# A hybrid attention and state-space layer: normalising the inputs before the conditioning is known, and a written order for the first two query units

## The chip, the core and the metric

One core of a Trainium2 chip runs the whole kernel. The metric is the device time of one launch in microseconds, the median of several runs.

## The reference, cut to what matters

The kernel computes one layer of a diffusion backbone over 1024 latent tokens of width 1024 and 256 context tokens. The part that the change touches is the start: the conditioning vector gives a shift and a scale per channel, the inputs are RMS-normalised and modulated, and the result is projected to queries, keys and values.

```
mod = (silu(c) @ ada_w + ada_b)
sh1, sc1, g1, sh2, sc2, g2 = split(mod, 6)
y = x * rsqrt(mean(x * x) + EPS)
h = (y * norm1_w) * (1.0 + sc1) + sh1
p = h @ w_in            # queries, keys, values, gates, state-space inputs
```

Everything behind it (rotary embedding, neighbourhood attention, a state-space scan in both directions, output projection, gated MLP with a depthwise convolution, final norm) is the same in both kernels.

## The kernel before, in words

All tensors are kept with the channels on the partitions: the input x is 8 channel tiles of 128 by 1024 tokens (`xt`), loaded in two halves of 512 tokens. Matrices are float32. For the large products each operand is split into a high part (`hh`, `wh`, in the fp32r format) and a low part (`hl`, `wl`: the rest), and three products (high by high, high by low, low by high) are added in PSUM.

The start has five kinds of work.

- **Norm.** ScalarE squares the 8 tiles of a half (L150, tiles `sq_x`), VectorE adds them up (L152, `sqa_x`), TensorE sums over the partitions (L154, `stat_x`). `rstd_rows` (L93) takes the root and the reciprocal, and a product with a matrix of ones (L105) spreads the inverse norm over the partitions in PSUM (`rbt`, one bank for each half).
- **Conditioning.** The product of the two conditioning vectors (latent and context) with `ada_w` is made in eight blocks of 256 columns. A block (`ada`, L157) loads 1 MB of weights (L159, `adaw`), makes eight products (L163, `adap`), copies the result to SBUF on ScalarE (L166, `adas`), and brings it onto the partitions with two small products (L169, `mp`). VectorE adds the bias (L172, `mod`, `modc`). Blocks 4 to 7 are scales, 0 to 3 shifts. A scale and a shift block together give the constants of a **pair** of channel tiles (L192, `scl`).
- **Modulation.** For each pair and half, `norm` (L174) makes `ny` = x times scale times inverse norm on VectorE (L176), `hh` = `ny` plus shift on ScalarE (L177) and `hl` = `ny` plus shift minus `hh` on VectorE (L178).
- **Weights.** `load_w` (L75) loads 512 KB for a unit of 128 output columns (`ws`), rounds it to `wh` on ScalarE (L79) and takes the rest `wl` on VectorE (L80).
- **Units.** `fm_unit` (L237) makes one unit: 8 channel tiles, three products each, two halves of 512 tokens, so 48 products (L90, `fu_qk`). There are eight query and key units. The products of `early` units run tile by tile as `hh` and `hl` become ready.

Nothing in the code fixes the order between these kinds: a scheduler places each engine's instructions when the program is built, and each engine then takes its own in that order. The weight loads of the conditioning have 4 buffers (`adap`), so that the loads of the last blocks wait for products of the first. All loads of the start are issued from one queue, SyncE's.

```
        for i in range(4):
            ada(4 + i)
            if i == 0:
                load_x(1)
            ada(i)
            if i < 3:
                pre[i] = load_w(A["wf"][8 + i], KT, P, f"qk0{i}")
```

## Time and profile before

| | |
|---|---|
| median of 3 runs | 1399.26 us (1398.8 to 1403.24) |
| the profiled execution | 1398.01 us |
| its span on the core | 1396.3 us |
| TensorE busy (matmuls) | 1330.7 us, 95% |
| VectorE, ScalarE, GpSimd busy | 854.9, 627.9, 307.9 us |
| share of the chain that ended last | TensorE 78%, DMA 8%, VectorE 5%, ScalarE 4% |

The chain that ended last is followed back from the last instruction, at each step to what released it. The first 60 us hold the work that the change touches. A line "x4" stands for four instructions that follow each other; the bracket at its end is the time for which the engine stood idle before it, and what ended that.

### The profile page before, as it was taken

The page shows a single profiled execution, that of the slowest core. Times are in us where ns is not written, and L with a number is a line of the kernel's source. Part 1 is how long each engine was busy: PE and PEld are TensorE (multiplying, and loading weights), DVE is VectorE, ACT ScalarE, POOL GpSimd, SP SyncE. Part 2 cuts the span into 40 slices and gives each one's busy share as a digit, 9 for nine tenths or more (in the row PEclk, how much of TensorE's full clock was granted, in tenths as well). Part 3 has the DMA queues.
Part 4 walks back from the last instruction along what each step waited for, and adds up shares of the span by engine and source line. Part 5 has one row for each costly group of instructions (what it writes and reads, how often), then busy time and mean ns, then how long its engine had stood idle before and what let it go on. Part 6 is the DMA issues. An engine that isn't in the chain of part 4 may idle for free.

```text
span 1396.3 us, 20022 instructions
## 1 busy us (share of the span) xinstructions
PE 1330.7 (95%) x7539; PEld 1118.8 (80%) x7539; DVE 854.9 (61%) x1343; ACT 627.9 (45%) x1052; POOL 307.9 (22%) x297
## 2 busy tenths in 40 slices
PE   5999999999989999999989999999999998999996
PEld 3788998889878787777887888888888877878885
DVE  5684246742377766548877655565656685585663
ACT  5441224332155558536646443454444554364441
POOL 0010000023657852000222222222222111201210
PEclk9999999999999999999999999999999999999998
DMA  9564675521697687343858676766667777677772
GB/s 370 217 166 123 162 238 196 192 91 49 190 256 207 206 228 255 107 138 119 201 119 198 160 187 153 176 159 150 162 156 174 235 245 187 160 219 206 186 179 74
DMA packets 118160, 251.02 MB, mean 180 GB/s; under 512 B 11944, under 2 KB 37288, under 8 KB 116784
## 3 DMA queue, kind: packets, MB, share of 16 engines
q1 hardware_dynamic: 92576, 197.58, 44.4%
q0 software_dynamic: 25488, 52.18, 20.1%
q8 instruction: 59, 0.97, 0.3%
q14 instruction: 37, 0.30, 0.1%
HBM read 212.16 MB, written 37.55 MB: 179 GB/s over the span
## 4 chain that ended last, share of the span: by engine, by line
PE 78%; DMA 8%; DVE 5%; ACT 4%; issue 2%; POOL 2%; SPq 0%; DVEq 0%; POOLq 0%; ACTq 0%
PE u L871 28%; PE pd L90 8%; PE fu_qk L90 6%; PE fu_x L90 6%; PE tu_v L90 4%; PE tu_z L90 3%; PE oc L90 3%; PE av L666 2%; PE os L90 2%; PE pm L1040 2%; PE pt L648 2%; PE oa L90 1%; DMA seg<-cum_d 1%; PE s L627 1%; PE fu_c L90 1%
## 5 line engine op out<-in xcount | busy, mean ns | idle before, releaser
L871 PE MATMUL u<-op,whu 128*128 128x512 f32 (+1 forms) x760 | 227.2, 382 | 1.7 <-DVE op L827 0.9
L871 PEld LDWEIGHTS u<-op,whu 128*128 128x128 f32 x760 | 140.1, 190 | 32.6 <-DVE op L827 1.1
L863 ACT ACTIVATE whu<-as 128x512 fp32r<-128x512 f32 x115 | 67.7, 625 | 173.9 <-PE u L871 166.0
L844 POOL DMA_DIRECT2D as<-in_w_up x69 | 66.3, 988 | 357.5 <-DMA as<-in_w_up 153.7
L871 PE MATMUL u<-op,wlu 128*128 128x512 f32 (+1 forms) x380 | 144.0, 380 | 0.0
L871 PE MATMUL u<-opx,whu 128*128 128x512 f32 (+1 forms) x384 | 110.2, 378 | 1.7 <-ACT whu L863 1.1
L864 DVE TENSOR_TENSOR wlu<-as,whu 128x512 fp32r<-128x512 f32 x115 | 76.0, 686 | 25.9 <-ACT whu L863 25.7
L871 PEld LDWEIGHTS u<-op,wlu 128*128 128x128 f32 x380 | 72.1, 190 | 14.9
L871 PEld LDWEIGHTS u<-opx,whu 128*128 128x128 f32 x384 | 69.6, 188 | 17.7 <-ACT whu L863 2.9
L90 PE MATMUL pd<-opx,wh_dn 128*128 128x512 f32 x256 | 81.3, 399 | 0.7 <-ACT wh_dn L79 0.6
L894 DVE TENSOR_TENSOR xa<-u,yz 128x512 f32<-128x512 f32 (+1 forms) x24 | 15.5, 646 | 98.2 <-PE u L871 98.2
L871 PE MATMUL u<-opx,wlu 128*128 128x512 f32 (+1 forms) x192 | 71.7, 376 | 0.0
L639 ACT ACTIVATE pr<-pr,mx 128x640 f32<-128x640 f32 x64 | 52.8, 825 | 39.3 <-DVE mx L638 39.2
L638 DVE CUSTOM_DVE_ANT_0 pr<-s,tabt 128x640 f32<-128x640 f32 x64 | 52.0, 818 | 20.2 <-PE s L628 16.1
L666 PE MATMUL av<-pts,vp 128*64 128x128 f32 x640 | 55.3, 285 | 5.8 <-ACT pts L650 5.3
L851 POOL DMA_DIRECT2D yz<-in_w_up x46 | 53.8, 1202 | 31.1 <-ACT yz L850 29.5
L90 PEld LDWEIGHTS pd<-opx,wh_dn 128*128 128x128 f32 x256 | 47.8, 189 | 12.6 <-ACT wh_dn L79 1.4
L871 PE MATMUL u<-opz,whu 128*128 128x512 f32 (+1 forms) x192 | 56.3, 376 | 1.2 <-ACT yz L886 1.2
L650 ACT ACTIVATE pts<-pt 128x640 f32<-128x640 f32 x64 | 43.8, 695 | 29.9 <-PE pt L648 19.7
L666 PEld LDWEIGHTS av<-pts,vp 128*64 128x64 f32 x640 | 40.5, 139 | 18.4 <-ACT pts L650 8.6
L648 PE MATMUL pt<-cst,pr 128*128 128x128 f32 x320 | 48.6, 283 | 5.5 <-ACT pr L639 2.6
L90 PE MATMUL pd<-opx,wl_dn 128*128 128x512 f32 x128 | 50.8, 398 | 1.9 <-DVE wl_dn L80 1.8
(644 smaller groups left out, 3574.8 us busy)
## 6 DMA issues: line engine op xcount, KB each, us to landing
as<-in_w_up SPq DMA_DIRECT2D x69, 256.0 KB, 4.0
as<-in_w_up POOLq DMA_DIRECT2D x69, 256.0 KB, 3.9
yz<-in_ada_wt SPq DMA_DIRECT2D x32, 512.0 KB, 4.5
ws_dn<-in_w_down SPq DMA_DIRECT2D x32, 448.0 KB, 4.0
as<-in_w_up SPq DMA_DIRECT2D x23, 512.0 KB, 5.8
yz<-in_w_up POOLq DMA_DIRECT2D x46, 256.0 KB, 5.8
g_d<-xa POOLq DMA_DIRECT2D x22, 512.0 KB, 4.6
tabt<-in_tab SPq DMA_DIRECT2D x48, 192.0 KB, 5.2
```

Source lines behind the costliest of these rows:

```text
L90: pe.matmul(out[:, t0:t1], st(a, k), mv(b, k, t0, t1), start=k == 0 and p == 0, stop=k == kend - 1 and p == 2, **kw)
L638: dve.tensor_tensor_reduce(pr, ps[:, lo:lo + 640], tabt[m % 2][:, 384 * j:384 * j + 640], -1.0, BIG, OP.add, OP.min, mx)
L639: act.activation(pr, pr, AF.Exp, bias=mx, scale=-1.0, accum_out=sm[:, n % 8:n % 8 + 1])
L648: pe.transpose(pt[:, i * P:(i + 1) * P], pr[:, i * P:(i + 1) * P], ident)
L650: act.activation(pts, pt[:, 0:640], AF.Copy)
L666: pe.matmul(av[64 * j:64 * j + 64, cb], vt, pp[j][:, i * P:(i + 1) * P], start=i == 0, stop=i == 4, skip_group_check=True)
L844: pool.dma_start(t, d, accum_op=OP.add)
L851: pool.dma_start(t, d, accum_op=OP.add)
L863: act.activation(h, src, AF.Copy)
L864: dve.tensor_tensor(l, src, f32(h), OP.subtract)
L871: mm = pe.matmul(ps[:, t0:t1], aops[n, o][a][:, k], bops[o][b][:, k, t0:t1], start=first and o < 5 and (t0 == 0 or n == 2), stop=end, skip ...
L1040: pe.matmul(dst[o], aops[n, o][a][:, k], sops[o][b][:, k], start=k == i == 0 and (o in (0, 2, 4) or o > 4 and first), stop=k == 3 and i == ...
```

## The change

1. `unit` multiplies the tiles of a half by the inverse norm in place, all eight at once and before the conditioning is needed (L214 of the changed kernel). The modulation is then `hh` = scale times y plus shift in one ScalarE instruction (L221); a second ScalarE instruction takes the shift off again (`nt`, L222), and VectorE makes `hl` = y times scale minus `nt` (L223). A negated shift (`neg`, L198) is added for it.
2. The first two query units are taken out of the loop. Their products are issued in pieces of one pair and one half (`query`, six products), and `in_turn` makes every TensorE instruction of the start follow the one written before it: the order on TensorE is the order of the text.
3. The conditioning loads are issued by `ada_load` in a written order, in six buffers. The tiles `ch` and `cl` of the context are allocated later.
4. The third unit's weights, and later ones, are loaded and split after the last conditioning load and the last `hh` and `hl`.

```diff
--- before.py
+++ after.py
@@ -108,19 +108,15 @@
...
-    ch = hxc.tile([P, KT, TC], FR, name="ch")
-    cl = hxc.tile([P, KT, TC], FR, name="cl")
...
-        adap = p0.enter_context(tc.tile_pool(name="adap", reuse_waits="tile", bufs=4))
+        adap = p0.enter_context(tc.tile_pool(name="adap", reuse_waits="tile", bufs=6))
...
+        def ada_load(i):
+            for b in (4 + i, i):
+                adaw[b] = adap.tile([P, KT, 256], FP, tag="ada", name=f"adaw{b}")
+                held["load"] = sp.dma_start(adaw[b], A["ada_w"][b]).ins
...
+        ada_load(0)
...
+        def mm(*a, **kw):
+            last[0] = pe.matmul(*a, **kw).ins
+
+        def in_turn(fn, *a):
+            if last[0] is None:
+                return fn(*a)
+            with tc.issue_after(last[0]):
+                return fn(*a)
...
-        def norm(src, rb, a, b, oh, ol, kt, n, key):
-            y = wk0.tile([P, n], FP, tag=f"ny{n // P}", name=f"ny_{key}{kt}", bufs=n // P)
-            dve.scalar_tensor_tensor(y, src[:, kt], a, rb, OP.mult, OP.mult)
-            act.activation(oh[:, kt], y, AF.Identity, bias=b)
-            dve.scalar_tensor_tensor(ol[:, kt], y, b, f32(oh[:, kt]), OP.add, OP.subtract)
...
+        def shift_scale(i):
+            for b in (4 + i, i):
+                in_turn(ada, b)
+            dve.tensor_scalar(neg[:, 2 * i:2 * i + 2], mod[:, 2 * i:2 * i + 2], -1.0, None, OP.mult)
...
+        def unit(h):
+            c = halves[h]
+            for kt in range(KT):
+                dve.tensor_tensor(xh[h][:, kt], xh[h][:, kt], rbt[:, c], OP.mult)
+
+        def norm(i, h):
+            c = halves[h]
+            for kt in (2 * i, 2 * i + 1):
+                y, a, b = xh[h][:, kt], scl[:, 0, kt:kt + 1], mod[:, kt:kt + 1]
+                t = wk0.tile([P, 512], FP, tag="nt", name=f"nt_x{h}{kt}", bufs=4)
+                held["high"] = act.activation(hh[:, kt, c], y, AF.Identity, scale=a, bias=b).ins
+                act.activation(t, f32(hh[:, kt, c]), AF.Identity, bias=neg[:, kt:kt + 1])
+                held["low"] = dve.scalar_tensor_tensor(hl[:, kt, c], y, a, t, OP.mult, OP.subtract).ins
+
+        early = [mmp.tile([P, T], FP, tag="mm", name=f"fu_qk0{u}") for u in range(2)]
+
+        def query(u, i, h):
+            wt, c = pre[u], halves[h]
+            for k in (2 * i, 2 * i + 1):
+                for p, (a, b) in enumerate(((0, 0), (0, 1), (1, 0))):
+                    mm(early[u][:, c], wt[a][:, k], (hh, hl)[b][:, k, c], start=k == 0 and p == 0,
+                       stop=k == KT - 1 and p == 2)
...
+        rows(0)
+        shift_scale(0)
+        pre[0] = load_w(A["wf"][8], KT, P, "qk00")
+        load_x(1)
+        ada_load(1)
+        unit(0)
+        norm(0, 0)
+        queries((0,), 0, (0,))
+        shift_scale(1)
+        pre[1] = load_w(A["wf"][9], KT, P, "qk01")
+        ada_load(2)
+        rows(1)
+        norm(1, 0)
+        queries((0,), 1, (0,))
+        queries((1,), 0, (0,))
+        unit(1)
+        norm(0, 1)
+        queries((1,), 1, (0,))
+        ada_load(3)
+        shift_scale(2)
+        norm(1, 1)
+        queries((0, 1), 0, (1,))
+        norm(2, 0)
+        queries((0, 1), 1, (1,))
+        norm(2, 1)
+        shift_scale(3)
+        queries((0, 1), 2, (0, 1))
+        for h in range(2):
+            norm(3, h)
+        queries((0, 1), 3, (0, 1))
+        with after("load", "high", "low"):
+            pre[2] = load_w(A["wf"][10], KT, P, "qk02")
...
-                pq.append(fm_unit(wt, hs, T, mmp, "mm", f"qk{blk}{f2}"))
+                pq.append(early[f2] if blk == 0 else fm_unit(wt, hs, T, mmp, "mm", f"qk{blk}{f2}"))
```

The order that the scheduler then gives each engine is shown at three places. **VectorE**, from the end of the first half's norm (`dg`) on. Before:

```order
L101 TENSOR_TENSOR dg_x_152<-cst,rst_x_149 128x512
L172 TENSOR_TENSOR mod<-mp_168,vec 128x2
L172 TENSOR_TENSOR modc<-mp_168,vec 128x2
L192 SCALAR_TENSOR_TENSOR scl<-mod,vec 128x2
L192 SCALAR_TENSOR_TENSOR scl<-modc,vec 128x2
L176 SCALAR_TENSOR_TENSOR ny_x_203<-xt,scl,rbt 128x512
L176 SCALAR_TENSOR_TENSOR ny_x_207<-xt,scl,rbt 128x512
```

In the changed kernel (the rows of the second half's sums, `sqa_x_274`, that stand between are part of it):

```order
L101 TENSOR_TENSOR dg_x_154<-cst,rst_x_151 128x512
L214 TENSOR_TENSOR xt<-xt,rbt 128x512 x8
L191 TENSOR_TENSOR mod<-mp_168,vec 128x2
L191 TENSOR_TENSOR modc<-mp_168,vec 128x2
L80 TENSOR_TENSOR wl_qk_194<-ws_qk_192,wh_qk_193 128x1024
L173 TENSOR_TENSOR sqa_x_274<-sqa_x_274,sq_x_276 128x512
L191 TENSOR_TENSOR mod<-mp_184,vec 128x2
L191 TENSOR_TENSOR modc<-mp_184,vec 128x2
L201 SCALAR_TENSOR_TENSOR scl<-mod,vec 128x2
L201 SCALAR_TENSOR_TENSOR scl<-modc,vec 128x2
L173 TENSOR_TENSOR sqa_x_274<-sqa_x_274,sq_x_279 128x512
L198 TENSOR_SCALAR neg<-mod 128x2
```

Behind these stand four more sums and then the first `hl`. Eight multiplications and one weight split moved ahead of the first scale. **TensorE**, from the second conditioning block's sums on; before (`fu_qk_448` and `fu_qk_497` are the first two units):

```order
L169 MATMUL mp_266<-sel,adas_264 128x2 x2
L163 MATMUL adap_273<-adaw_271,sc 32x256 x8
L90 MATMUL fu_qk_497<-hh,wh_qk_290 128x512
L90 MATMUL fu_qk_448<-hh,wh_qk_196 128x512
L90 MATMUL fu_qk_448<-hl,wh_qk_196 128x512
L90 MATMUL fu_qk_497<-hh,wh_qk_290 128x512
L90 MATMUL fu_qk_497<-hl,wh_qk_290 128x512
L169 MATMUL mp_284<-sel,adas_282 128x2 x2
L163 MATMUL adap_315<-adaw_313,sc 32x256 x8
```

In the changed kernel (`fu_qk_121` is the first unit):

```order
L158 MATMUL fu_qk_121<-hh,wl_qk_194 128x512
L158 MATMUL adap_228<-adaw_202,sc 32x256 x8
L158 MATMUL mp_239<-sel,adas_237 128x2 x2
L158 MATMUL adap_244<-adaw_204,sc 32x256 x8
L158 MATMUL mp_255<-sel,adas_253 128x2 x2
L158 MATMUL stat_x_273<-ones_63,sqa_x_274 128x1 x4
L158 MATMUL fu_qk_121<-hh,wh_qk_193 128x512
L105 MATMUL rbt<-dg_x_304,cst 128x512
L158 MATMUL fu_qk_121<-hl,wh_qk_193 128x512
```

Where unit products stood between a block's eight products and the two small ones that need its copy, the two now follow each other. **ScalarE**, around the copies of the third pair's blocks in the changed kernel:

```order
L221 ACTIVATE hh<-xt,mod,scl 128x512 x2
L222 ACTIVATE nt_x_335<-hh,neg 128x512
L221 ACTIVATE hh<-xt,mod,scl 128x512
L222 ACTIVATE nt_x_339<-hh,neg 128x512
L221 ACTIVATE hh<-xt,mod,scl 128x512
L222 ACTIVATE nt_x_388<-hh,neg 128x512
L222 ACTIVATE nt_x_392<-hh,neg 128x512
L185 ACTIVATE adas_362<-adap_353 128x256
```

Eight passes over the second half's first two pairs now stand ahead of the copy `adas_362`. Behind the query and key units the engines' order is the same in both kernels but for a stretch of the MLP's up-projection, where groups of 512 and 256 columns (line 871, `u`) change places.

## Rows read from the trace of the kernel before

**Rows 1.** The page, part 1: busy time of each engine.

```profile
PE 1330.7 (95%) x7539; PEld 1118.8 (80%) x7539; DVE 854.9 (61%) x1343; ACT 627.9 (45%) x1052; POOL 307.9 (22%) x297
```

**Rows 2.** Busy time by stretch: stretch, length, each engine, granted clock, DMA share, GB/s.

```profile
0.00:11.70 11.70, 0.00 (x0) 0.00 (x0) 5.21 (x10) 7.38 (x11) 0.20 (x4) 1.00 0.83 301
11.70:34.30 22.60, 17.11 (x98) 10.15 (x98) 13.63 (x28) 11.17 (x20) 0.00 (x0) 1.00 1.01 404
34.30:57.50 23.20, 23.16 (x156) 17.39 (x156) 17.15 (x38) 7.42 (x14) 0.00 (x0) 1.00 0.63 248
57.50:140.00 82.50, 82.50 (x396) 68.58 (x396) 50.31 (x64) 28.47 (x51) 5.72 (x8) 1.00 0.56 148
```

**Rows 3.** The same view, first 57.5 us, the units' products (fu_qk) alone.

```profile
0.00:57.50 57.50, 19.17 (x73) 13.30 (x74) 0.00 (x0) 1.00 0.82 320
```

**Rows 4.** The chain that ended last, from 55 us: start, length, what.

```profile
57.52 17.79 PE fu_qk L90 x76
```

**Rows 5.** Timeline of TensorE: start, length, line, operation, count, idle before.

```profile
11.70 1.86 PE L154 MATMUL stat_x<-ones,sqa_x 128*128 128x1 f32 x8 [11.70 <-DVE sqa_x L152]
13.50 1.93 PE L163 MATMUL adap<-adaw,sc 128*32 128x256 f32 x16
15.36 2.08 PE L105 MATMUL rbt<-dg_x,cst 128*128 128x512 f32 x2
...
20.86 1.93 PE L163 MATMUL adap<-adaw,sc 128*32 128x256 f32 x16 [2.78 <-DMA adaw<-in_ada_w]
25.36 1.02 PE L169 MATMUL mp<-sel,adas 128*128 128x2 f32 x4 [2.56 <-ACT adas L166]
26.52 1.84 PE L154 MATMUL stat_x<-ones,sqa_x 128*128 128x1 f32 x8
...
30.75 1.78 PE L105 MATMUL rbt<-dg_x,cst 128*128 128x512 f32 x2
...
32.80 1.07 PE L163 MATMUL adap<-adaw,sc 128*32 128x256 f32 x16
...
41.52 1.07 PE L163 MATMUL adap<-adaw,sc 128*32 128x256 f32 x16
...
47.51 0.50 PE L169 MATMUL mp<-sel,adas 128*128 128x2 f32 x4
```

**Rows 6.** Timeline of VectorE, the same columns.

```profile
6.14 5.51 DVE L152 TENSOR_TENSOR sqa_x<-sqa_x,sq_x 128x512 f32<-128x512 f32 x7 [4.93 <-ACT sq_x L150]
...
18.12 0.16 DVE L172 TENSOR_TENSOR mod<-mp,vec 128x2 f32<-128x2 f32 x1 [3.26 <-PE mp L169]
...
24.55 1.22 DVE L80 TENSOR_TENSOR wl_qk<-ws_qk,wh_qk 128x1024 fp32r<-128x1024 f32 x1
...
28.98 0.69 DVE L101 TENSOR_TENSOR dg_x<-cst,rst_x 128x512 f32<-128x512 f32 x1
...
39.61 2.74 DVE L178 SCALAR_TENSOR_TENSOR hl<-ny_x,mod,hh 128x512 fp32r<-128x512 f32 x4
...
42.65 2.72 DVE L176 SCALAR_TENSOR_TENSOR ny_x<-xt,scl,rbt 128x512 f32<-128x512 f32 x4
```

**Rows 7.** Timeline of ScalarE, the same columns.

```profile
38.35 2.57 ACT L177 ACTIVATE hh<-ny_x,mod 128x512 fp32r<-128x512 f32 x4 [0.95 <-DVE mod L172]
42.72 0.38 ACT L166 ACTIVATE adas<-adap 128x256 f32<-128x256 f32 x1 [1.80 <-PE adap L163]
```

**Rows 8.** Transfers issued from 33 to 34.3 us: count, size, us to landing.

```profile
adaw<-in_ada_w SPq DMA_DIRECT2D x1, 1024.0 KB, 10.3
```

**Rows 9.** Busy time by stretch (columns of rows 2) at the MLP's start.

```profile
702.00:704.00 2.00, 2.00 (x12) 2.00 (x11) 2.00 (x5) 0.18 (x1) 0.86 (x1) 0.50 1.00 208
```

**Rows 10.** Timeline of TensorE in the up-projection.

```profile
710.92 0.38 PE L871 MATMUL u<-op,whu 128*128 128x256 f32 x1 [0.40 <-ACT op L826]
...
712.18 0.39 PE L871 MATMUL u<-op,whu 128*128 128x256 f32 x1 [0.88 <-DVE op L827]
...
714.35 1.03 PE L871 MATMUL u<-opx,whu 128*128 128x256 f32 x4 [0.60 <-ACT whu L863]
```

More of the change, by code (lines that the diff above doesn't have):

```diff
@@ L168, in ada @@
             for f in range(2):
[L169 removed]
+                mm(mp[:, f], sb[:, f * P:(f + 1) * P], sel, start=True, stop=True)
             c0 = 2 * b
@@ L193, in hymba @@
                                          vec[:, V_N1 + 2 * i:V_N1 + 2 * i + 2], OP.add, OP.mult)
-            for h in range(2):
-                if i == 0 and h:
-                    rstd_rows(mmp, wk0, stats(wk0, xh[1], 4, "x1"), 4, "mm", "x1", "sqa4", rb=rbx[1])
-                for kt in (2 * i, 2 * i + 1):
-                    c = slice(512 * h, 512 * h + 512)
-                    norm(xh[h], rbx[h], scl[:, 0, kt:kt + 1], mod[:, kt:kt + 1], hh[:, :, c], hl[:, :, c], kt, 512, f"x{h}")
+        rbt = mmp.tile([P, T], FP, tag="mm", name="rbt")
@@ new lines, in hymba, with rows @@
+        halves = [slice(512 * h, 512 * h + 512) for h in range(2)]
+        def rows(h):
+            sums = in_turn(stats, wk0, xh[h], 4, f"x{h}")
+            rstd_rows(mmp, wk0, sums, 4, "mm", f"x{h}", "sqa4", rb=rbt[:, halves[h]])
+        def unit(h):
[10 more added lines that the diff above has]
+                held["low"] = dve.scalar_tensor_tensor(hl[:, kt, c], y, a, t, OP.mult, OP.subtract).ins
@@ L201, in hymba @@
+    cl = hxc.tile([P, KT, TC], FR, name="cl")
     hs = (hh, hl)
@@ L286, in hymba @@
             for f2 in range(2):
-                wt = pre[2 * blk + f2] if 2 * blk + f2 in pre else load_w(A["wf"][8 + 2 * blk + f2], KT, P, f"qk{blk}{f2}")
+                wt = pre.get(2 * blk + f2)
+                if not wt:
+                    with after("load", "high", "low"):
+                        wt = load_w(A["wf"][8 + 2 * blk + f2], KT, P, f"qk{blk}{f2}")
                 wts.append(wt)
-                pq.append(fm_unit(wt, hs, T, mmp, "mm", f"qk{blk}{f2}"))
+                pq.append(early[f2] if blk == 0 else fm_unit(wt, hs, T, mmp, "mm", f"qk{blk}{f2}"))
             pA, pB = pq
```

39 lines of the change are left out of this document (20 added, 19 removed).

## The prediction, made blind

> **What bounds the kernel now.** I read the views from the whole to the part. The page says that TensorE works for 95% of the span [rows 1], so the first question is where it does not. The busy time by stretch answers for the start [rows 2]: nothing until 11.70 us, 17.11 of 22.60 us until 34.3, then 23.16 of 23.20 and 82.50 of 82.50. From 34.3 us to 140 us TensorE has no gap worth naming, and from 57.5 us on it does nothing but units and what belongs to them. So the change can win only what TensorE idles before 34.3 us: the first 11.70 us wait for the first half's sums, which the change leaves alone, and 22.60 - 17.11 = 5.5 us lie behind them. Anything that opens a gap behind 34.3 us is lost in full, because the chain that ended last runs through these very products [rows 4].
>
> By 57.5 us 73 of the units' products are done [rows 3], beside all eight conditioning blocks. The scheduler gets there by putting products of the first two units between a block's eight products and the two small ones that need its copy: the block at 41.52 us has its `mp` only at 47.51 us, and TensorE works in between [rows 5].
>
> **What is removed.** The loads of the last conditioning block are issued near 34 us and land 10.3 us later [rows 8], near 44 us. In the new order all eight stand ahead of the third unit's weights. The queue moves 404 GB/s in 11.70 to 34.3 us [rows 2], so a block of 1.05 MB takes 2.6 us; x, eight blocks and two weights are about 13.6 MB, which ends near 38 us (an estimate from that rate). The first pair's second block can start behind the first block's `mp` instead of at 20.86 us after a wait of 2.78 us for its load [rows 5]. That wait and the 2.56 us for its copy go; they are most of the 5.5 us.
>
> **What is added, step by step.** I walk TensorE in its new order, with row durations. Until 17.4 us (the end of `rbt`, 15.36 + 2.08 [rows 5]) nothing changes.
> - *First product.* Block 4's `mp`, block 0, its copy and `mp` are done by about 21.2 us, with 0.5 us of waiting for the copy. But the first `hh` needs `scl`, and on VectorE eight multiplications by the norm stand ahead of it. The nearest rows are the `ny` passes, which also read PSUM: four in 2.72 us, 0.66 us each [rows 6]. So 8 x 0.66 = 5.3 us, then `wl` 1.22, one sum 0.7 and five tiny operations 0.5: 17.4 + 7.7 = 25.1 us. `hh` takes 0.7 [rows 7]. The first product starts at 25.8 us: **4.6 us of waiting**.
> - *Second product.* It needs `hl`, and in the written order nothing may pass it. Ahead of `hl` VectorE has five sums, each bound to the one before (seven took 5.51 us, 0.79 each [rows 6]), then `hl` itself, 0.7: 25.2 + 4.7 = 29.9 us at the most, 29.1 if the sums go at their bare 0.7. TensorE is free at 26.3: **3.0 us**.
> - *Blocks 5 and 1.* Block, copy, `mp`, block, copy, `mp` now follow each other. A copy is 0.38 us and starts 0.13 us behind its block (42.72 against 41.52 + 1.07) [rows 5, 7], and the product behind it follows at 0.1: 0.6 us, twice: **1.2 us**. The same for blocks 7 and 3: **1.2 us**, and for block 2: **0.5 us**.
> - *Second half's norm.* From the end of `stat_x` at 28.36 us to the end of `dg` at 29.67 us it took 1.3 us [rows 5, 6], beneath a conditioning block. Now one unit product (with 0.3 us of its own wait) stands there, and the root stands behind two `hh` on ScalarE: **1.9 us**.
> - *Block 6.* Its copy stands behind eight ScalarE passes, `hh` and `nt`. Four `hh` take 2.57 us [rows 7], so eight end 4.9 us behind the first multiplied tile of the second half, near 48 us, where TensorE has done its 17 products (17.79 us for 76, 0.234 each [rows 4]) and the block by about 46.4: **1.8 us**.
>
> The sum is 0.5 + 4.6 + 3.0 + 1.2 + 1.2 + 0.5 + 1.9 + 1.8 = 14.7 us of waiting, against 5.5: **9.2 us more**. A second working gives nearly the same: conditioning ends near 60.3 us instead of 57.5, with 48 products done (6, 18 and 24 by the written order) instead of 73: 2.8 + 25 x 0.234 = 8.7 us.
>
> **What comes for nothing.** The sixteen `nt` passes are 16 x 0.62 = 9.9 us of ScalarE, which works for 18.6 of the 45.8 us between 11.7 and 57.5 us [rows 2]; the part on the path is the 1.8 us above. The later loading of the third unit's weights stays beneath the products of pair 3; without that cover it would cost the split, 1 + 1.2 us. Rope and context work are placed alike. `hh` now has a scale in memory beside its bias, which no row shows; I take the row of `hh` with a bias alone, with nothing and twice its 0.7 us as ends.
> The Trainium skill, ScalarE: Activation LUTs, What ACT_TABLE_LOAD costs, puts about 93 ns on each per-partition operand; by that the eight passes ahead of block 6's copy, four of them `hh`, and the first `hh` would add some 0.5 us, and the sum would be 9.7 us. No row of this trace shows it.
>
> **The clock.** The granted clock reads 1.00 in these stretches [rows 2], but the same block takes 1.93 us at 13.50 and 20.86 and 1.07 us at 32.80 [rows 5]. I read the early rows as the lower of the two levels, 1.2 GHz, and those from 32.8 us on as 2.4 GHz; ahead of the rise TensorE worked without a gap from 26.5 us. In the new order its longest unbroken work before 40 us is about 4 us (29.1 to 33.3). Either that is enough: then the second half's `stat_x` and `rbt` come at the high level, each some 0.9 us less, and five more unit products at the low one, 0.2 us each: -0.8, in all +8.4. Or the rise waits for the dense products behind 42 us: block 1 costs 0.9 more and twelve products 0.2 each, while block 6's wait shrinks by 1.8 because TensorE comes later itself: +1.5, in all +10.7. I take +9.5 between the two, as the rows don't tell them apart.
>
> **The up-projection.** Groups of `u` change places there. The waits near by are 0.40, 0.88 and 0.60 us [rows 10]: 1.9 us either way, taken as nothing.
>
> **The sum.** The profiled execution took 1398.01 us, of which 1396.3 are the span. 1398.0 + 9.5 = 1407.5. The median of the three runs lies 1.25 us above that execution, so I forecast 1408.8 us.
>
> **The rivals.**
> *The waits close up (faster).* Nothing but TensorE's own work need limit it once the loads are there. If `hl` came with `hh` and each copy hid beneath something, the start would lose only its first 11.70 us, and the gain is the old 5.5 us: 1393.8 us. For it speak the earlier loads. Against it stands the order itself: eight multiplications ahead of the first scale, five sums ahead of the first `hl`. It decides at the first `hl`: faster needs the new waits to stay under 1.3 us in all (5.5 less 4.2), and the first product alone has 4.6. I give it 6%.
> *Half of it (no change).* If VectorE takes its multiplications faster than the `ny` rows and TensorE is at the high level from the start, the first two waits shrink to half (3.8 less), the low level's cost goes (some 4 us, as three blocks, two sums and a spread each give back 0.9), and 1 to 3 us are left: about 1401. 15%.
> *The clock falls back (slower still).* At the MLP's start a stretch of 2 us shows the granted clock at 0.50 with TensorE busy throughout [rows 9], behind gaps of the kind that the new order puts around blocks 6, 2, 7 and 3. Each such time would cost half its length, 1 to 2 us here, two of them up to 4: 1412 us. 17%.
> The Trainium skill, TensorE: Matmul & The Clock Gate, Why this matters for your kernels, warns of just this: gaps between bursts of matmuls send the engine back to its lower level.
> *The change does not do what it says.* The order on TensorE is written and shows in the built program, so this has no chance of its own.
>
> **How the numbers follow.** 0.3% of 1399.26, 4.2 us, is what a measurement can tell from no change: faster is below 1395.1, slower above 1403.5. The forecast (both cases of the clock, 1407.7 to 1410, and 1.9 us about them for the up-projection) has 62%, the fall-back 17%: slower 0.79. No change 0.15, faster 0.06. The range leaves out the faster case, the lower part of no change and the far end of the fall-back: 1401 to 1413.
>
> **What the changed profile would show.** Right: TensorE's first unit product at 25 to 27 us, a wait of about 3 us for `hl` behind it, waits of 0.4 to 0.7 us for `adas` ahead of `mp`, some 14 to 15 us idle between 11.7 and 61 us where there were 5.5, and the last unit of keys ending 8 to 11 us later; all behind that moved by the same. Wrong: unit products without a gap from 27 us, or the eight multiplications in much under 5 us, or block times near 1.07 us from the first on.

## The result, and the profile after

The changed kernel takes 1407.75 us (median of 14 runs, 1402.12 to 1417.54); the kernel before took 1399.1 us in the same comparison (14 runs, 1389.21 to 1406.66). The ratio is 1.007, 95% interval 1.0046 to 1.0093: slower by some 8.7 us. The forecast was 1408.8 us, with 0.79 on slower.

The profiled execution of the changed kernel is the longest of its 14 (1417.54 us, span 1415.8), so the span alone misleads; the start has to be read by itself. The milestone is the first product of the value units (`tu_v`), since all query and key units stand ahead of it. Its rows by the view of one tile (number, shortest, median and longest in ns, first and last start), the kernel before first, then the changed one:

```profile
L90 PE MATMUL tu_v<-wh_v,hh x128: 279/283/289, 142.3 to 194.4; 128*128 128x264 f32 x128
L90 PE MATMUL tu_v<-wh_v,hh x128: 279/283/289, 152.7 to 204.8; 128*128 128x264 f32 x128
```

That is 142.3 and 152.7 us, 10.4 us later. The busy time by stretch answers to [rows 2] (length, then busy time of TensorE, its weight loads, VectorE, ScalarE, GpSimd, then the granted clock, DMA share and GB/s):

```profile
11.70:34.30 22.60, 13.06 (x80) 7.33 (x84) 14.57 (x29) 10.64 (x19) 0.00 (x0) 0.77 1.01 406
34.30:57.50 23.20, 20.41 (x112) 14.14 (x112) 13.94 (x34) 14.84 (x24) 0.00 (x0) 0.78 0.56 222
57.50:140.00 82.50, 81.49 (x404) 66.22 (x403) 48.52 (x67) 32.62 (x57) 5.76 (x8) 1.00 0.56 147
```

TensorE idles 9.5, 2.8 and 1.0 us in these three stretches, where it idled 5.5, 0.04 and nothing. Beside that the granted clock falls to 0.77 and 0.78 where it read 1.00. (In the first of the stretches that is not all a loss: until 32 us the kernel before works at the lower level too, at 1.93 us for a block [rows 5], though its column reads 1.00.) So the 10.4 us have two parts, and the timeline of TensorE shows both (start, length, line, operation, count, and in brackets the idle time ahead of it and what ended that):

```profile
11.91 1.87 PE L158 MATMUL stat_x<-ones,sqa_x 128*128 128x1 f32 x8 [11.91 <-DVE sqa_x L173]
...
17.51 1.07 PE L158 MATMUL adap<-adaw,sc 128*32 128x256 f32 x16
19.65 0.61 PE L158 MATMUL mp<-sel,adas 128*128 128x2 f32 x4 [1.06 <-ACT adas L185]
25.45 0.79 PE L158 MATMUL fu_qk<-hh,wh_qk 128*128 128x512 f32 x1 [5.20 <-ACT hh L221]
28.81 0.80 PE L158 MATMUL fu_qk<-hl,wh_qk 128*128 128x512 f32 x1 [2.56 <-DVE hl L223]
...
31.24 1.94 PE L158 MATMUL adap<-adaw,sc 128*32 128x256 f32 x16
...
39.39 2.08 PE L105 MATMUL rbt<-dg_x,cst 128*128 128x512 f32 x2 [1.07 <-DVE dg_x L101]
...
48.13 0.61 PE L158 MATMUL mp<-sel,adas 128*128 128x2 f32 x4 [0.50 <-ACT adas L185]
48.67 1.07 PE L158 MATMUL adap<-adaw,sc 128*32 128x256 f32 x16
```

First part, the waits: 5.20 us for the first `hh`, 2.56 for the first `hl`, a copy of 0.50 us ahead of each `mp`. Second part, the pace: a block takes 1.07 us at 17.51, but 1.94 us at 31.24 behind the two long waits, and 1.07 again at 48.67. TensorE had reached its higher level (2.4 GHz) at 17 us and went back to 1.2 GHz; in the kernel before, the blocks at 32.80 and behind are all at 1.07 [rows 5]. The same view in finer stretches:

```profile
25.40:28.80 3.40, 0.79 (x1) 0.29 (x1) 3.09 (x6) 3.34 (x6) 0.00 (x0) 0.50 1.03 424
28.80:32.00 3.20, 3.19 (x13) 1.75 (x17) 2.35 (x3) 0.69 (x1) 0.00 (x0) 0.50 0.99 412
...
40.00:44.00 4.00, 4.00 (x9) 2.49 (x8) 3.16 (x7) 1.77 (x3) 0.00 (x0) 0.50 0.43 171
44.00:48.00 4.00, 3.63 (x28) 2.22 (x26) 4.00 (x7) 3.93 (x7) 0.00 (x0) 1.00 0.00 0
48.00:56.00 8.00, 7.37 (x40) 5.65 (x41) 3.06 (x11) 5.38 (x10) 0.00 (x0) 0.79 0.69 263
```

Between 40 and 44 us TensorE is busy throughout and does 9 instructions; between 44 and 48 us it does 28 in 3.63 us. The chain that ended last (start, length, what) carries this into the time:

```profile
41.47 5.16 PE fu_qk L158 x17
...
50.85 7.24 PE fu_qk L158 x24
```

A unit product costs 0.30 us there, against 17.79 / 76 = 0.234 us in [rows 4].

VectorE, the engine that both long waits point to, shows why they are where they are (same columns as TensorE's timeline):

```profile
17.28 4.87 DVE L214 TENSOR_TENSOR xt<-xt,rbt 128x512 f32<-128x512 f32 x8 [2.21 <-PE rbt L105]
...
22.21 1.22 DVE L80 TENSOR_TENSOR wl_qk<-ws_qk,wh_qk 128x1024 fp32r<-128x1024 f32 x1
...
24.08 0.16 DVE L201 SCALAR_TENSOR_TENSOR scl<-mod,vec 128x2 f32<-128x2 f32 x1
...
25.01 3.08 DVE L173 TENSOR_TENSOR sqa_x<-sqa_x,sq_x 128x512 f32<-128x512 f32 x4
28.01 0.75 DVE L223 SCALAR_TENSOR_TENSOR hl<-xt,scl,nt_x 128x512 fp32r<-128x512 f32 x1
```

Eight multiplications by the inverse norm and the split of a weight stand ahead of the first scale, and five sums of squares between that scale and the first `hl`: one at 24.21 us and the four in the rows. On ScalarE the groups of the first 62 us (count, busy us, mean ns of one, idle ahead):

```profile
L221 ACT ACTIVATE hh<-xt,mod,scl 128x512 fp32r<-128x512 f32 x12 | 9.1, 806 | 4.5 <-DVE xt L214 2.7 <-DVE mod L191 1.8
L222 ACT ACTIVATE nt_x<-hh,neg 128x512 f32<-128x512 f32 x12 | 8.0, 710 | 0.0
```

### The profile page after: what moved, and what is told of

Its sections match the earlier page's. It is cut to its first block, busy times and chain, and to the rows that moved or that the text cites. A ratio compares the mean times of both kernels' runs of the same rounds, so it can differ in the third digit from the quotient of the medians.

```text
span 1415.8 us, 20045 instructions
## 1 busy us (share of the span) xinstructions
PE 1335.3 (94%) x7539; PEld 1122.0 (79%) x7539; DVE 852.9 (60%) x1347; ACT 639.6 (45%) x1068; POOL 307.6 (22%) x297
## 4 chain that ended last, share of the span: by engine, by line
PE 75%; DMA 10%; DVE 5%; ACT 3%; POOL 3%; issue 3%; SPq 0%; DVEq 0%; POOLq 0%; ACTq 0%
PE u L949 29%; PE fu_x L90 6%; PE pd L90 6%; PE fu_qk L90 5%; PE tu_v L90 4%; PE oc L90 3%; PE tu_z L90 2%; DMA seg<-cum_d 2%; PE av L744 2%; PE fu_qk L158 2%; PE os L90 2%; PE pt L726 2%; PE oa L90 1%; PE s L705 1%; DMA as('d', 0, 0)1_9666<-in_w_down 1%
```

## The experiments

Twelve experiments follow: eleven new kernels, and the change once more. Three numbers are read from each. The first is the start of `tu_v`. The second is TensorE's idle time from 11.7 to 154.4 us, from two rows of the busy time by stretch: for the changed kernel, as an example, 49.30 - 36.47 and 93.40 - 92.90, together 13.3 us.

```profile
11.70:61.00 49.30, 36.47 (x224) 22.96 (x224) 28.94 (x67) 25.86 (x44) 0.00 (x0) 0.79 0.73 291
61.00:154.40 93.40, 92.90 (x461) 77.78 (x458) 55.35 (x71) 36.74 (x62) 5.76 (x8) 1.00 0.51 138
```

The kernel before has 49.30 - 43.76 = 5.5 us in the first of them and nothing in the second:

```profile
11.70:61.00 49.30, 43.76 (x268) 30.35 (x269) 33.50 (x70) 21.84 (x40) 0.00 (x0) 1.00 0.76 302
```
(The first sums start between 11.7 and 12.3 us, so up to 0.6 us of a number is chance.) The third is what the difference of the first leaves over that of the second. The work is the same, so this is the pace at which it is done. For the changed kernel: 10.4 - (13.3 - 5.5) = 2.6 us. Where useless products fill the idle time, the second and third number say nothing and are left out.

| kernel | ratio to before, 95% interval | tu_v, us | against before | of it idle | of it pace |
|---|---|---|---|---|---|
| the change | 1.007 [1.0046, 1.0093] | 152.7 | +10.4 | +7.8 | +2.6 |
| 12: the change, second execution | one run, 1407.64 us | 154.4 | +12.1 | +5.5 | +6.6 |
| 1: order left to the scheduler | 1.0053 [1.0031, 1.0075] | 149.5 | +7.2 | +5.2 | +2.0 |
| 2: the change with the old norm | 1.0095 [1.0066, 1.0125] | 153.1 | +10.8 | +4.9 | +5.9 |
| 3: before with the new loads alone | 1.0022 [0.9996, 1.0049] | 145.8 | +3.5 | +2.4 | +1.1 |
| 4: before with the new norm alone | 1.0111 [1.0068, 1.0154] | 156.1 | +13.8 | +8.7 | +5.1 |
| 5: before, idle time filled | 0.999 [0.9967, 1.0014] | 141.8 | -0.5 | | |
| 6: the change, idle time filled | 1.008 [1.0053, 1.0107] | 148.8 | +6.5 | | |
| 7: the change, copies hidden | 1.0035 [1.0008, 1.0063] | 149.1 | +6.8 | +2.0 | +4.8 |
| 8: the change, two tiles first | 1.0069 [1.0045, 1.0093] | 150.6 | +8.3 | +3.7 | +4.6 |
| 9: 7 and 8 together | 1.0033 [1.0012, 1.0053] | 146.3 | +4.0 | +2.7 | +1.3 |
| 10: 3, with block 5 ahead of the sums | 0.9984 [0.9959, 1.0009] | 141.9 | -0.4 | -0.6 | +0.2 |
| 11: 7 with the old norm | one run, 1403.38 us | 150.4 | +8.1 | +2.7 | +5.4 |

The last three columns come from one profiled execution of each kernel, and two executions of the changed kernel (the first two rows) differ by 1.7 us in the start of `tu_v` and by 4.0 us in the pace. Differences of that size between rows are not shown to be more than chance. The whole times have intervals of 3 to 6 us to either side. They hold the change of the start in every row but one: number 6 as a whole is 0.8% or 11.2 us longer than before (7.4 to 15.0), and only 6.5 us later at `tu_v`.

### The parts of the change, one undone or one alone

**1, the order left to the scheduler.** In the changed kernel:

```diff
         def in_turn(fn, *a):
-            if last[0] is None:
-                return fn(*a)
-            with tc.issue_after(last[0]):
-                return fn(*a)
+            return fn(*a)
```

> The changed kernel with one thing undone: TensorE's instructions are no longer bound to the written order, the scheduler places them as in the kernel before. Loads, buffers, norm and the early query products stay. Measure: when the first product of the value units (tu_v) starts, 142.3 us before and 152.7 after, and TensorE's waits between 11.7 and 61 us, 5.5 and 12.8 us. Order theory (the written order makes the waits, as the prediction has it): a block's eight products or other unit products slide into the waits for hl and for the copies; waits 6 to 9 us, tu_v at 146 to 149, the whole some 5 us faster than after. Norm theory (hh and hl are late whatever the order is, because eight multiplications stand ahead of the first scale): waits stay above 11 us, tu_v at 151 to 153. Clock theory (the gaps hold TensorE at its lower level): with half the gaps gone the level rises once, near 32 us, and stays; tu_v at 144 to 146, and a unit product takes 0.23 us throughout from there.

Measured: 149.5 us, idle 10.7 us, between the theories: 3.2 us come back, a little less than the order theory asks for and more than the norm theory allows; the clock theory's 144 to 146 is out. So most of the loss, 7.2 of 10.4 us, is still there without the written order. The wait for the first `hl` shrinks from 2.56 to 0.70 us because block 5 slides ahead of it, as said; the wait for the first `hh` stays:

```profile
26.23 0.79 PE L158 MATMUL fu_qk<-hh,wh_qk 128*128 128x512 f32 x1 [4.78 <-ACT hh L218]
26.95 1.94 PE L158 MATMUL adap<-adaw,sc 128*32 128x256 f32 x16
29.59 0.79 PE L158 MATMUL fu_qk<-hl,wh_qk 128*128 128x512 f32 x1 [0.70 <-DVE hl L220]
```

**2, the old norm in the new order.** In the changed kernel (the calls of `unit` and the negated shift go as well):

```diff
-                held["high"] = act.activation(hh[:, kt, c], y, AF.Identity, scale=a, bias=b).ins
-                act.activation(t, f32(hh[:, kt, c]), AF.Identity, bias=neg[:, kt:kt + 1])
-                held["low"] = dve.scalar_tensor_tensor(hl[:, kt, c], y, a, t, OP.mult, OP.subtract).ins
+                dve.scalar_tensor_tensor(t, y, a, rbt[:, c], OP.mult, OP.mult)
+                held["high"] = act.activation(hh[:, kt, c], t, AF.Identity, bias=b).ins
+                held["low"] = dve.scalar_tensor_tensor(hl[:, kt, c], t, b, f32(hh[:, kt, c]), OP.add, OP.subtract).ins
```

> The changed kernel with its written order, loads and buffers, but with the modulation of the kernel before: per tile one VectorE pass x * scale * norm, one ScalarE pass + shift, one VectorE pass for the rest; no multiplication of all inputs ahead, no negated shift. Same measures. Norm theory: the first unit product starts 3.5 to 4 us earlier (near 21.8 instead of 25.45), nothing is lost later, tu_v at 145 to 148. Order theory: the first product comes as early, but TensorE then waits as long at other places of the written order (second products, copies, second half): waits 10 to 13 us in all, tu_v at 150 to 152. Clock theory: as the order theory, with a low level again behind each gap.

Measured: the first product starts at 22.7 us, 2.8 us earlier, and `tu_v` at 153.1, no earlier at all (a little behind the order theory's 150 to 152). The waits move to the second half and the level stays low with them:

```profile
22.69 0.74 PE L158 MATMUL fu_qk<-hh,wh_qk 128*128 128x512 f32 x1 [1.76 <-ACT hh L221]
...
36.46 2.07 PE L105 MATMUL rbt<-dg_x,cst 128*128 128x512 f32 x2 [1.36 <-DVE dg_x L101]
40.13 0.79 PE L158 MATMUL fu_qk<-hh,wh_qk 128*128 128x512 f32 x1 [1.59 <-ACT hh L221]
42.01 0.80 PE L158 MATMUL fu_qk<-hl,wh_qk 128*128 128x512 f32 x1 [1.09 <-DVE hl L222]
```

The norm theory falls for this order: the old norm gives nothing back (0.4 us the other way, within the 1.7 us between two executions of the changed kernel).

**3, the new loads alone.** In the kernel before, six buffers, and:

```diff
+        ada_load(0)
...
             ada(4 + i)
-            if i == 0:
-                load_x(1)
             ada(i)
             if i < 3:
                 pre[i] = load_w(A["wf"][8 + i], KT, P, f"qk0{i}")
+            if i == 0:
+                load_x(1)
+            if i < 3:
+                ada_load(i + 1)
```

> The kernel before with the new order of loads alone (all conditioning blocks ahead, x's second half behind the first pair, six buffers); the scheduler places TensorE's work, the norm is the old one. If the waits of the kernel before for its loads (2.78 us for one block) are what the change can win: waits 2 to 3.5 us instead of 5.5, tu_v at 139 to 141. Rival, the loads were hidden or another wait takes their place (the copy, the clock rising later): tu_v at 141.5 to 143. If the new order of loads itself costs: above 143.

Measured: 145.8 us; the third case, the loads alone cost 3.5 us at `tu_v` (the whole is 0.2% longer, with an interval that includes no change, and cannot confirm it). The first product starts at 23.0 us instead of 30.2, but x's second half lands later, and TensorE waits for its sums with block 5 behind them in its queue:

```profile
27.76 1.84 PE L158 MATMUL stat_x<-ones,sqa_x 128*128 128x1 f32 x8 [3.93 <-DVE sqa_x L156]
29.53 1.93 PE L166 MATMUL adap<-adaw,sc 128*32 128x256 f32 x16
```

**4, the new norm alone.** In the kernel before, `unit` of each half behind its inverse norm, `neg`, and:

```diff
-            dve.scalar_tensor_tensor(y, src[:, kt], a, rb, OP.mult, OP.mult)
-            act.activation(oh[:, kt], y, AF.Identity, bias=b)
-            dve.scalar_tensor_tensor(ol[:, kt], y, b, f32(oh[:, kt]), OP.add, OP.subtract)
+            act.activation(oh[:, kt], y, AF.Identity, scale=a, bias=b)
+            act.activation(t, f32(oh[:, kt]), AF.Identity, bias=neg[:, kt:kt + 1])
+            dve.scalar_tensor_tensor(ol[:, kt], y, a, t, OP.mult, OP.subtract)
```

> The kernel before with the new norm alone (all eight tiles of a half multiplied by the inverse norm ahead, then scale and shift on ScalarE, the shift taken off again, one VectorE pass for the rest); loads and order as before. Norm theory: hh and hl come late whatever the order, VectorE's multiplications and ScalarE's doubled passes stand ahead of the copies that free the conditioning blocks; tu_v at 146 to 150. Order theory (the norm costs only where the order is written): tu_v at 142 to 144.

Measured: 156.1 us, worse than the whole change and beyond what either theory allowed. The conditioning ends late (its last shift at 68.2 us, 57.6 before), and from 60 us on TensorE waits, by the table of waits (in all, times, longest), for what follows from it:

```profile
PE stat_c L154 <- DVE sqa_c L152: 2.3, 1, 2.3
PE fu_qk L90 <- DVE rp L307: 1.7, 1, 1.7
PE fu_qk L90 <- DVE hl L179: 1.6, 2, 1.0
```

Block copies stand behind the `hh` passes on ScalarE there (one at 59.73 us behind four of them, 2.94 us); that this is what makes the conditioning late is likely and not shown, as no run moves them. This kernel's `nt` has two buffers and the changed kernel's four, but its `nt` waits for `hl` only 0.9 us in all until 75 us. So the parts do not add up: loads +3.5, norm +13.8, both together with a free order +7.2 (number 1, which also keeps the query products in pieces and the third unit's weights held back; these two were not run alone).

### Idle time against pace

**5 and 6, the idle time filled.** Both kernels get useless products of zeros on TensorE, in 5 ahead of the first half's sums, in the wait for the second block and in that for its copy, in 6 ahead of the sums and in the waits for the first `hh` and `hl`. The cut shows 6, with products of 96x96 by 96; 5 takes 128x128 by 256:

```diff
+        def warm(n):
+            t = m1p.tile([P, 256], FP, tag="m1", name="warm")
+            for _ in range(n):
...
+                    mm(t[:96, :96], wz, wz, start=True, stop=True)
...
+        warm(42)
         rows(0)
...
+        warm(27)
         queries((0,), 0, (0,))
```

> The kernel before with useless products added on TensorE, where it idles: 16 of 128x128 by 128x256 zeros ahead of the first half's sums, 11 in the wait for the second conditioning block, 6 in the wait for its copy; everything else as before. Measures: the start of tu_v (142.3 us before) and the granted clock. In the first experiments the level rose after some 6 us of unbroken work (the block at 18.1 us takes 1.07 us) and was low again behind waits of 2.6 and 3.9 us. Clock theory (the waits keep TensorE at its lower level until 32 us): the first block takes 1.07 instead of 1.93 us, so do the sums (0.95) and the spread (1.1); what is ahead of the loads' wait is absorbed by it, the stretch of 25 to 32 us (6.3 us of work) gives back some 3 us; tu_v at 138.5 to 140.5, the whole 2 to 4 us faster. Rival, wait theory (other engines and loads set the start, TensorE's level in it costs nothing): tu_v at 141.8 to 142.8. If the useless products get in the way (queued ahead of work that is ready): above 143.

> The changed kernel with useless products added on TensorE in its three longest waits (42 of 96x96 zeros ahead of the first half's sums, 27 in the wait for the first hh, 13 in that for the first hl); nothing else changed. It parts the waits of the written order from the clock that they cost. After: tu_v at 152.7 us, waits of 12.8 us behind the first 11.9, and several stretches at the lower level until 56 us. Clock theory: at the higher level from the first sums on, each block 1.07, each unit product 0.23 us; the work behind the first hl comes some 4 us earlier, and 2 us more are given back between 40 and 56 us; tu_v at 145 to 148. Order theory (the waits are the cost; at the higher level TensorE only waits longer): tu_v at 150 to 152.7, real waits and useless products together 15 us or more.

Measured, 5: the level is high from the first sums on, and it gains 0.5 us. What TensorE does faster it waits for behind 30 us, where it never waited before:

```profile
13.42 1.07 PE L151 MATMUL adap<-adaw,sc 128*32 128x256 f32 x16 [0.59 <-DMA adaw<-in_ada_w]
...
32.59 0.49 PE L90 MATMUL fu_qk<-hh,wh_qk 128*128 128x512 f32 x1 [1.05 <-ACT hh L196]
...
36.46 0.50 PE L90 MATMUL fu_qk<-hl,wh_qk 128*128 128x512 f32 x1 [1.68 <-DVE hl L197]
```

So in the kernel before the wait theory holds: loads, VectorE and ScalarE set the start, and TensorE's low level until 32 us is free. Measured, 6: 148.8 us, 3.9 us less than the first execution of the change and 5.6 less than the second; the clock theory asked for 145 to 148, the order theory for 150 and more, so it lies between. The level fell once more for block 4 and `rbt` (1.94 and 1.70 us) before the second fill, and again at `rbt` of the second half (2.07 us). What stays, 6.5 us, are waits that no pace removes: seven copies with 4.1 us, and the fills themselves, which stand in the waits for `hh` and `hl`. The whole time does not show the gain: 1.008 against 1.007 for the change. So the price of the pace is seen at `tu_v` of one execution and is not confirmed by the runs of the whole.

**12, the change once more.** The kernel is unaltered.

> The changed kernel once more, unaltered, for the spread of one execution's numbers. Its profiled execution was the longest of its runs, with tu_v at 152.7 us and 1252.9 us from there to the last rb_o product, where the kernel before has 1243.3. If what comes behind the start is the same work at a varying pace: tu_v within 1.5 us of 152.7, and the rest nearer to 1243 to 1248 us. If the change costs something behind the start as well: the rest at 1252 us again.

Measured: 154.4 us, a little more than 1.5 from the first. Two executions of one kernel divide their loss differently: here the level rises late, so TensorE arrives late and waits less (5.5 us more than before, not 7.8) but works slower (6.6, not 2.6).

```profile
18.03 1.93 PE L158 MATMUL adap<-adaw,sc 128*32 128x256 f32 x16
...
25.66 0.79 PE L158 MATMUL fu_qk<-hh,wh_qk 128*128 128x512 f32 x1 [4.17 <-ACT hh L221]
...
34.83 1.93 PE L158 MATMUL adap<-adaw,sc 128*32 128x256 f32 x16
```

Behind the start, from the first `tu_v` to the last spread of the norms at the end (`rb_o`), it takes 1395.3 - 154.4 = 1240.9 us. The first execution took 1405.6 - 152.7 = 1252.9, the kernel before 1385.6 - 142.3 = 1243.3, and the eleven other kernels lie between 1238.2 (number 3) and 1250.2 (number 5), whatever was done to the start. So the change costs nothing that shows behind the start; the 9 us more of its first profiled execution are within what changes from run to run, and the whole, +8.7 us (6.4 to 13.0), asks for nothing beyond the start.

### The waits of the written order, one by one

**7, the copies hidden.** The changed kernel, with query products written between a block and its `mp`:

```diff
-        queries((0,), 0, (0,))
-        shift_scale(1)
+        shift_scale(1, [(query, 0, 0, 0, (0,))], [(query, 0, 0, 0, (1,))])
...
-        queries((1,), 1, (0,))
-        shift_scale(2)
+        shift_scale(2, [(query, 1, 1, 0)], [(query, 0, 0, 1)])
...
-        shift_scale(3)
-        queries((0, 1), 2, (0, 1))
+        shift_scale(3, [(query, 1, 1, 1)], [(query, 0, 2, 0)])
+        queries((0,), 2, (1,))
+        queries((1,), 2, (0, 1))
```

> The changed kernel with one thing altered in its written order: query products stand between a block's eight products and its mp (three behind block 5, three behind block 1, six each behind blocks 6, 2, 7 and 3), so block 5 also comes ahead of the first product. Norm, loads, buffers and VectorE's work as in the change. The waits that should go: the copies of blocks 5, 1, 6, 2, 7 and 3 (0.5 us each, 3 us), most of the 2.56 us for the first hl (block 5's products and copy are ahead, so hl is there), and 1.9 of the 5.2 us for the first hh (block 5 stands in it): 7.5 us. Order theory: waits of TensorE behind 11.9 us fall from 12.8 to 5 to 7 us, tu_v from 152.7 to 145.5 to 148. Rival, the late norm sets the pace (what is won ahead is waited for at the second half's sums, its inverse norm or the scales of pair 2): tu_v at 150 to 152.5. Rival, the clock: waits go as said, but the level stays low as long as before, tu_v at 148 to 150.

Measured: 149.1 us, in the band of the clock rival. The idle time falls from 13.3 to 7.5 us, by 5.8 us, nearly as the order theory says; but the pace costs 4.8 us, so 3.6 us are left of it. Against the second execution it is 5.3 us, 3.5 of idle time and 1.8 of pace, so how the gain divides depends on the execution that it is held against. The waits in 12 to 62 us, as a table:

```profile
PE adap L158 <- DVE scl L207: 3.8, 1, 3.8
PE fu_qk L158 <- DVE hl L229: 1.7, 1, 1.7
PE mp L158 <- ACT adas L185: 1.0, 2, 0.5
PE rbt L105 <- DVE dg_x L101: 0.7, 1, 0.7
```

Seven waits for copies (4.1 us in the changed kernel) have become two. Block 5 did not go into the old wait for `hh` as expected: it starts at 24.79 us behind the 3.8 us of the first row. That row names `scl`; in numbers 9 and 11 the same block waits for its load, until 25.09 and 24.70 us.

**8, two tiles first.** The changed kernel, with the other six multiplications behind the first `hl`:

```diff
-        unit(0)
+        unit(0, (0, 1))
         norm(0, 0)
+        with after("low"):
+            unit(0, range(2, KT))
```

> The changed kernel with one thing altered on VectorE: of the first half's eight multiplications by the inverse norm only the two of pair 0 stand ahead of the first scale, the other six come behind the first hl. The first product should start 6 x 0.61 = 3.7 us earlier, at 21.8 us, whatever comes after. Norm theory (the multiplications ahead of the first scale are the price): tu_v falls by as much, to 148.5 to 149.5. Order theory (TensorE then only waits elsewhere in its written order: for block 5's load and copy, for the second half's sums that now stand behind six multiplications): of the 3.7 us at most 2 stay, tu_v at 150.5 to 152.5.

Measured: the first product at 23.39 us, 2.1 us earlier and not 3.7, because `hh` then waits for the shift behind block 0's `mp` (done at 21.63 us) and for four squares ahead of it on ScalarE (until 22.5 us); `tu_v` at 150.6, 2.1 us less, at the edge of the order theory. The second execution of the change (number 12), where block 0 and all blocks until 36 us take 1.93 us as here, is the better partner: against it the first product is 2.3 us earlier, block 6 2.6 (45.67 against 48.30) and `tu_v` 3.8, so the 2.3 us are kept.

```profile
20.62 1.01 PE L158 MATMUL mp<-sel,adas 128*128 128x2 f32 x4 [0.50 <-ACT adas L185]
23.39 0.79 PE L158 MATMUL fu_qk<-hh,wh_qk 128*128 128x512 f32 x1 [1.76 <-ACT hh L221]
26.80 0.80 PE L158 MATMUL fu_qk<-hl,wh_qk 128*128 128x512 f32 x1 [2.62 <-DVE hl L223]
```

**9, both.** The edits of 7 and 8 together.

> Both alterations together: query products between a block and its mp, and two of the eight multiplications first. If the waits are as the prediction counts them and independent, the two gains add up: tu_v at 143.5 to 146. If the multiplications matter only where TensorE has nothing else to do, the second alteration adds less than 1 us to the first: within 1 us of the first run of this call. Neither theory expects it below the kernel before (142.3).

Measured: 146.3 us, 0.3 above the band. The gains at `tu_v` add up: 3.6 + 2.1 = 5.7 from single edits, 6.4 together. It is still 4.0 us behind the kernel before, and the largest wait left is of another kind, block 5's load:

```profile
25.09 1.93 PE L158 MATMUL adap<-adaw,sc 128*32 128x256 f32 x16 [4.53 <-DMA adaw<-in_ada_w]
```

**11, the copies hidden and the old norm.** The edits of 7 and 2 together.

> The changed kernel with the query products between a block and its mp (as in the run with the copies hidden, tu_v at 149.1 us) and with the norm of the kernel before. With the scheduler free the new norm cost 149.5 - 145.8 = 3.7 us; with the change's own strict order it cost nothing (152.7 against 153.1). If the strict waits hid the norm's price, it shows again here: tu_v at 145 to 147.5. If the norm is free wherever the order is written: 148.5 to 150.

Measured: 150.4 us, a little above the second band: with the order written, the new norm costs nothing a second time (150.4 with the old, 149.1 with the new, within the 1.7 us between two executions). The theory that the strict waits hid its price does not come out: most of the copies' waits are gone here, and no price shows.

**10, the best arrangement of the parts.** To number 3 one thing more: block 5 stands in the program ahead of the second half's sums.

```diff
                 if i == 0 and h:
+                    for b in (5,):
+                        ada(b)
                     rstd_rows(mmp, wk0, stats(wk0, xh[1], 4, "x1"), 4, "mm", "x1", "sqa4", rb=rbx[1])
```

> The kernel before with the change's loads and buffers (as in the run with the loads alone, tu_v at 145.8 us), and one thing more: block 5 stands ahead of the second half's sums of squares in the program. In the run with the loads alone TensorE waited 3.93 us for those sums with block 5 queued behind them. Theory (the new loads lose only by that place in the queue): block 5 fills 1.9 us of the wait and its copy is no longer late; tu_v at 141 to 143.5, the whole within 0.2% of before. Rival (VectorE's sums and the norm set the pace of this stretch whatever TensorE does meanwhile): tu_v at 144.5 to 146. This is the arrangement of the parts of the change that comes nearest to beating the kernel before.

Measured: 141.9 us, the whole 0.9984 of before, 0.9959 to 1.0009: no difference that can be told. The wait of 3.93 us is gone; others, of 2.58, 1.14 and 0.72 us, stand in 17 to 25 us, and the idle time is 5.0 us against 5.5.

```profile
22.71 0.79 PE L90 MATMUL fu_qk<-hh,wh_qk 128*128 128x512 f32 x1 [2.58 <-ACT hh L180]
24.64 1.93 PE L166 MATMUL adap<-adaw,sc 128*32 128x256 f32 x16 [1.14 <-DMA adaw<-in_ada_w]
```

No version was found that beats the kernel before by more than the measurement can tell.

## Why the prediction was right, and which terms were not

The time was right (1407.75 against 1408.8 us), and so was the cause in kind: waits of TensorE at the places that the prediction named, all ahead of 64 us. The start costs 10.4 and 12.1 us in the two executions, against a forecast of 9.5; that it came so near is in part luck, as terms off in opposite directions made up for each other. The written order is not the whole of it: with the order left free 7.2 us remain (number 1), and the new loads alone cost 3.5 (number 3). By its steps:

- *First product.* Forecast at 25.8 us behind 4.6 us of waiting; measured 25.45 and 25.66 us behind 5.20 and 4.17. The multiplications took 4.87 us, the term had 5.3. Number 8 shows the cause: with six of them moved the product comes 2.1 us earlier. It does not come 3.7 us earlier: block 0's shift and ScalarE's squares are next, which the term did not name.
- *Second product.* 3.0 us forecast, 2.56 in both; the sums ahead of `hl` are in the rows above, and a product of another kind in between removes most of it (0.70 us in number 1).
- *Copies.* 0.5 + 1.2 + 1.2 + 0.5 forecast; a copy cost 0.50 us each time, and 1.06 once, when its block ran at the higher level and ScalarE was still at a square. Number 7 was to hide six of the seven waits and hides five.
- *Second half's norm.* 1.9 forecast, 0.21 + 1.07 and 0.73 measured. The root came behind two `hh` as the term said, but a unit product at the lower level (0.80 us) covered part of it.
- *Block 6.* 1.8 forecast, 0.50 and 0.52 measured. The term stood on TensorE being done by 46.4 us; it was done at 47.6, since 17 products took 5.16 us and not 4.0. The second case of the clock had named this very trade.
- *The sum of the waits.* 14.7 us forecast, 13.3 and 11.0 measured; above the 5.5 of before that is 7.8 and 5.5, not 9.2.
- *The clock.* This is the term that was mis-sized. It was taken at +0.3 us, between -0.8 and +1.5, with the waits that a slower TensorE shortens counted in. On the same terms the two executions gave 10.4 - 9.2 = +1.2 and 12.1 - 9.2 = +2.9 us. By itself the pace cost 2.6 and 6.6 us, while the waits came out 1.4 and 3.7 us below the 9.2: a slow TensorE comes later to what it would wait for. The second case of the clock had this trade (block 1 and twelve products slower, block 6's wait 1.8 us shorter); the second execution is close to it, with unit products at 0.63 us until 44.93 us and at 0.39 from 45.66. What both cases left out is that the level falls again. It does, in the first execution three times (seen at 25.45, 37.53 and 50.71 us), in the second once (at 52.01), so the rival in which the clock falls back had that part. Of the two places where it put a fall, around blocks 6 and 2 and around blocks 7 and 3, only the first shows one. Its 4 us would have been added to waits that are then shorter. Number 6 gives 3.9 to 5.6 us of the pace back at `tu_v`, but not in the whole. One sum in the rivals is off: three blocks, two sums and a spread at 0.9 us each are 5.4 us, not some 4; number 5 shows that in the kernel before the low level of the start costs 0.5 us.
- *What comes for nothing.* `nt` on ScalarE was counted at nothing beside block 6. In the written order this holds: numbers 2 and 11, without it, are not faster. It holds only there: with a free order, number 1 lies 149.5 - 145.8 = 3.7 us behind number 3, which has the old norm (and no products in pieces, no weights held back), and in the kernel before the new norm alone costs 13.8. What covers it in the written order stays open: the waits for the copies do not, as number 11 shows.
- *The loads.* They were booked as a gain, the 2.78 us for block 0 and the 2.56 for its copy. Both waits went, and number 3 shows that this was no gain: the later second half of x took 3.93 us for them. Number 10 shows the place of block 5 as the reason: moved ahead of those sums, it brings the start back to 141.9 us. The prediction never asked what is late next when x's second half moves behind blocks; the written order hid the omission, because it puts blocks 5 and 1 ahead of those sums.
- *A scale in memory.* Taken at nothing. `hh` with scale and bias in memory took 806 ns, four in a row 2.94 us [rows 7: 2.57 with the bias alone], 0.09 us each. The Trainium skill, ScalarE: Activation LUTs, What ACT_TABLE_LOAD costs, gives about 93 ns for such an operand; these rows agree.
- *Behind the start.* The up-projection's 1.9 us either way, taken as nothing, cannot be seen: the stretch behind `tu_v` varies between 1238.2 and 1252.9 us over all the profiled executions.

The Trainium skill, TensorE: Matmul & The Clock Gate, Why this matters for your kernels, warns of gaps between bursts; here the rows agree (1.07 us for a block at 17.51, 1.94 at 31.24 behind waits of 5.20 and 2.56 us). They also show falls without such gaps: the block at 48.67 us takes 1.07, and the unit products from 50.71 on take 0.63 at first, with no wait longer than 0.50 us since 40 us. That a lower level need not cost anything shows in number 5.

What stays open: how much of the 10.4 us is pace in a typical execution, since two gave 2.6 and 6.6; and how numbers 3 and 4 interact (together +7.2, the norm alone +13.8) was not followed further than the table of waits. The query products in pieces and the held-back weights were never run alone, so their share of the 7.2 us is not known.

## What to carry to other kernels

An order written by hand for one engine has to name, for every instruction in it, when its operands are ready on the other engines; here, unit products between a block and the product that needs its copy gave back 3.6 us of the start, more than undoing the new arithmetic did (nothing). Read the idle time and the pace as two columns of one account: fewer waits may come with a lower clock, and useless work that holds the clock up gains nothing worth naming where loads and other engines set the pace (0.5 us in number 5). Before counting a vanished wait as a gain, find what is late next: the loads removed a wait of 2.78 us and made one of 3.93.

## What was not expected

- The level is not a matter of the kernel alone. Of two executions of the changed kernel the one had block 0 at 1.07 us (17.51), the other at 1.93 (18.03) and all blocks so until 36 us.
- The granted clock's column must be read beside durations: for 36 to 42 us it reads 1.00 in the second execution, where `rbt` takes 2.07 us at 41.35, as at the lower level; here it falls below 1.00 only in stretches behind a first rise.

```profile
36.00:42.00 6.00, 4.77 (x22) 3.35 (x15) 1.94 (x7) 3.38 (x6) 0.00 (x0) 1.00 0.93 374
```

- At the higher level from its first product on, the kernel before gains 0.5 us. The slow rows of its start seemed to hold some 6.6: two sums of 0.8, three blocks of 0.86 (the third at 28.29 us), two spreads of 0.96 and 0.66, two `mp` of 0.4 (one at 17.23 us) [rows 5]. The rest turned into waits, of 1.05 and 1.68 us and earlier ones.
